# Other prices in a list scheduler: table loads, transfer landings and GpSimd's wake-up

## The chip, the cores and the metric

The kernel runs on one core of one Trainium2 chip. The metric is device microseconds of one execution. A core has five engines that run instruction streams of their own, each in order: TensorE (PE; its weight loads are shown apart as PEld), VectorE (DVE), ScalarE (ACT), GpSimd (POOL) and SyncE (SP), which in this kernel issues every transfer between DRAM and the core's memory (SBUF). TensorE writes to PSUM, of which the kernel uses eight banks of 128 x 512 floats.

## The reference

One layer of an encoder trunk, in float32, for a prompt of 1024 tokens and for 32 further tokens with a cache of 512 past ones; both share the weights.

```python
u = rmsnorm(h, g_pre) @ w_in                  # 1024 -> 4096: qA kA vA gA qB kB vB gB
# A: band attention, 8 heads of 64; a chunk of 64 queries reads its own chunk and 8 before it
s = q @ k.T * 64 ** -0.5 + bias_table[clip(k_pos - q_pos, -128, 128)]
oA = softmax(where(in_band, s, -1e30)) @ v
# B: stick-breaking attention, 8 heads of 64, strictly causal
z = q @ k.T * 64 ** -0.5
log_1m = where(causal, log_sigmoid(-z), 0)
after = reverse_cumsum(log_1m) - log_1m
oB = where(causal, exp(log_sigmoid(z) + after), 0) @ v
y = concat(oA * silu(gA), oB * silu(gB)) @ w_out
h = h + rmsnorm(y, g_post)
h = h + sigmoid(h @ w_ple_gate) * (p @ w_ple)
```

It returns `h` of both groups and their new keys and values.

## The kernel before

**Arithmetic.** Matmuls run on a rounded 32-bit type. To keep float32 precision, an operand is split into a high part (a rounding copy, mostly on ScalarE) and a low part (operand minus high part, on VectorE or GpSimd), and a product is the sum of two or three matmuls. In tile names `h` and `l` stand for these, as in `wTh` and `wTl`.

**Stages.** First the norm and transposes of the input (`ptx`) and a part of the `p @ w_ple` products (`ple`). Then the projections of `w_in`, one matmul group `mm_..` per 128 output columns and 352 tokens, woven together with the attention: 16 heads in eight pairs, in the order A0, B0, A1, B1, ... A3, B3. A head is named by group, pair and half: A01 is the second head of band pair 0. While the attention runs, GpSimd also forms sums of weight blocks and stores them to DRAM (`oB`, `gB` to `sum_dro`, `sum_drg`), for the two products at the end (`o`, `g`), which use a Strassen-like scheme with seven products. The projections of the gates (`mm_gA`, `mm_gB`) come behind the attention, then the rest of `ple`, then the output products, norms and gate.

**One head.** Its queries stand in eight tiles of 128. For tile i, TensorE computes scores into PSUM (`SA`, `SB`). A band head then has VectorE add the bias and find the minimum (`om<-SA,biasA`, `statA`), and ScalarE the exponential (`be<-om,statA`). A stick-breaking head has ScalarE's sigmoid (`om<-SB`), a running product on VectorE (the scan `om<-om,SB`) and a difference on GpSimd (`be<-om`). ScalarE keeps one function table at a time, so from an exponential to a sigmoid and back the program has a table load. The weights must then be transposed for the product with the values (`PVA`, `PVB`). For six tiles TensorE does that (`ptwA`, `ptwB`), with a cast `wTh<-ptw` on ScalarE and the rest `wTl<-ptw,wTh` on VectorE. Tiles 4 and 6 go another way: VectorE transposes squares of 32 x 32, SyncE stores the tile to DRAM (`swapA<-om`) and loads it back in four strips (`be<-swapA`), and then come the cast `wTh<-be` and the rest `wTl<-be,wTh`. So 32 such swaps lie in the kernel, two a head, and the second half of a head's `PV` product waits for both of its own.

**The order.** Nothing in the program is issued as it is written. Every call goes through a `Recorder`, which notes an `Op` with its engine, its predecessors (by the boxes of the tiles that it reads and writes) and a price from `cost`: the time that it keeps its engine (`busy`) and a delay until its result can be used (`late`). `order` then plays a list schedule. Each engine has a time from which it is free; the engine that can start first takes, of the instructions whose operands are there at that time, the one with the lowest key. The key is a class (for TensorE 0 for attention, 1 for projections that fill in) and the place in the recorded program. The finish of an instruction, plus `SEM` and for a reader on TensorE a `MARGIN` of 400 ns, sets when its readers are ready. `emit` writes out the instructions in the order in which they were taken. The buffers of the pools (three banks for scores, two for transposes, two for `mm`, one for `PV`) are given out in the same order. The prices therefore do not appear in the program; they only decide which instruction stands ahead of which on each engine. As every engine works in order, an instruction whose operands come later than planned holds up all that stand behind it on its engine.

For a transfer (`e == "SP"`), the model keeps SyncE busy for `ISSUE` and sends the data down one line of 320 bytes a ns, or slower where the runs are short.

All instructions in the profile have the line of the call in `emit` (L452 before), so they are told apart by tile names.

Of the kernel before, what the change touches and what calls it, by code (L numbers as in the profile page):

```python
# [8 lines left out]
F32 = mybir.dt.float32  # L9
F32R = mybir.dt.float32r  # L10
AF = mybir.ActivationFunctionType
# [161 lines left out]


class Op:
    __slots__ = ("eng", "what", "args", "kw", "key", "busy", "late", "ready", "left", "after", "at", "size", "shared")


LAND = {"PE": 165, "ACT": 0, "DVE": 0, "POOL": 0, "SP": 0, "CTL": 0}
SEM = 60  # L180
MARGIN = 400
ISSUE = 600
DMA_NS, DMA_RATE, DMA_MARGIN = 1500, 320.0, 2000
DVE_SET, POOL_SET = 137, 110


# [77 lines left out]
class Recorder:  # L264
# [35 lines left out]
    def node(self, eng, what, args, kw, after):  # L300
        o = Op()
        o.eng, o.what, o.args, o.kw, o.after = eng, what, args, kw, after
        o.key = (self.cls if eng == "PE" else self.low, len(self.ops))
        o.shared = False
        self.ops.append(o)
        return o

    def add(self, eng, what, args, kw):
        writes, reads = [], []
        method = what[1] if isinstance(what, tuple) else ""  # L310
        for i, a in enumerate(args):
            if isinstance(a, (View, Raw, Segments)):
                (writes if i == 0 or (method == "tensor_tensor_reduce" and i == 7) else reads).append(a)
        for k, a in kw.items():
            if isinstance(a, (View, Raw, Segments)):
                (writes if k in ("out", "accum_out") else reads).append(a)
        o = self.node(eng, what, args, kw, set())
        for mine, write in ((reads, False), (writes, True)):
            for v in mine:
                b = v.buf  # L320
                hit = False
                for other, box, wrote in b.uses:
                    if other is not o and (write or wrote) and all(p < y and x < q for (p, q), (x, y) in zip(v.box, box)):
                        o.after.add(other)
                        hit = True
                if b.pool is not None:
                    if not hit:
                        o.after.add(b.place)
                    b.pool.ops.append(o)
                b.uses.append((o, v.box, write))  # L330
        o.busy, o.late = self.cost(eng, method, args, kw, writes, reads)
        o.shared = eng == "POOL"
        if eng == "DVE":
            sbuf = [v for v in reads if isinstance(v, (View, Segments)) and not v.buf.psum and v.free() > 4]
            o.shared = len(sbuf) > 1 or (method == "tensor_copy" and len(sbuf) == 1 and not writes[0].buf.psum)

    @staticmethod
    def cost(eng, method, args, kw, writes, reads):

        out = writes[0] if writes else None  # L340
        n = out.free() if isinstance(out, View) else 1
        psum = any(isinstance(v, (View, Segments)) and v.buf.psum for v in reads)
        if eng == "PE":
            if method == "transpose":
                return (109 if args[1].shape[0] > 64 else 62), 165
            return max(109.0, 2.5 + 0.449 * args[2].free()) * (1 if args[2].buf.dtype == F32R else 4), 165
        if eng == "ACT":
            return (60 if psum else 95) + 0.83 * n + (190 if "accum_out" in kw else 0), 105
        if eng == "DVE":
            if method == "tensor_tensor_scan":  # L350
                return 120 + 2.1 * n, 85
            if method == "tensor_copy" and not psum:
                return 70 + 0.53 * n, 85
            if method == "scalar_tensor_tensor":
                return 125 + 1.04 * n, 85
            if method == "tensor_tensor_reduce":
                return 90 + 1.04 * n, 150
            return 70 + 1.04 * n, 85
        if eng == "POOL":
            if method == "tensor_tensor":  # L360
                if n == 1:
                    return 535, 40
                return 170 + (1.77 if out.buf.dtype == F32 else 2.15) * n, 40
            if method == "tensor_scalar":
                return 255 + 0.86 * n, 0
            return 100 + 0.82 * n, 0
        size, run = 4, 0
        for v in (out, args[1]):
            if isinstance(v, View) and v.buf.pool is not None:
                size, run = 4 * v.shape[0] * v.free(), 4 * v.shape[-1]  # L370
        return ISSUE, max(size / DMA_RATE, size / run * (8.5 + 0.0365 * run) / 16)


    def order(self):

        import heapq
        for place, old in self.turns:
            place.after.update(x[0] for x in old.uses)
        users = {id(o): [] for o in self.ops}
        for o in self.ops:  # L380
            o.left, o.ready = len(o.after), 0.0
            for a in o.after:
                users[id(a)].append(o)
        names = ("PE", "ACT", "DVE", "POOL", "SP", "CTL")
        free = dict.fromkeys(names, 0.0)
        soon = {e: [] for e in names}
        now = {e: [] for e in names}
        for o in self.ops:
            if not o.left:
                heapq.heappush(soon[o.eng], (0.0, o.key, id(o), o))  # L390
        out, port, line = [], 0.0, 0.0
        while len(out) < len(self.ops):
            best = None
            for e in names:
                if now[e]:
                    t = free[e]
                elif soon[e]:
                    t = max(free[e], soon[e][0][0])
                else:
                    continue  # L400
                if best is None or t < best[0]:
                    best = (t, e)
            t, e = best
            while soon[e] and soon[e][0][0] <= t:
                _, key, n, o = heapq.heappop(soon[e])
                heapq.heappush(now[e], (key, n, o))
            o = heapq.heappop(now[e])[2]
            if o.shared and e == "DVE" and port > t + DVE_SET:
                held = [x for x in now[e] if not x[2].shared]
                if held:  # L410
                    heapq.heappush(now[e], (o.key, id(o), o))
                    pick = min(held)
                    now[e].remove(pick)
                    heapq.heapify(now[e])
                    o = pick[2]
            o.at = t
            if e == "CTL":
                done = t
            elif e == "SP":
                free[e] = t + o.busy  # L420
                line = max(line, t + o.busy + DMA_NS) + o.late
                done = line + DMA_MARGIN
            else:
                if o.shared:
                    t = max(t, port - (DVE_SET if e == "DVE" else POOL_SET))
                    port = t + o.busy
                free[e] = t + o.busy
                done = t + o.busy + o.late
            out.append(o)
            for u in users[id(o)]:  # L430
                if u.eng == e and e != "SP":
                    r = t if e == "CTL" else free[e] if e == "PE" else done
                else:
                    r = done + (0 if u.eng == "CTL" else SEM + (MARGIN if u.eng == "PE" else 0))
                u.ready = max(u.ready, r)
                u.left -= 1
                if not u.left:
                    heapq.heappush(soon[u.eng], (u.ready, u.key, id(u), u))
        return out
# [18 lines left out]
def stream_step(  # L458
# [79 lines left out]
    def load_w(j):  # L538

        if j >= len(order) or j in raws:  # L540
            return
        kind, p = order[j]
        c0 = NAMES.index(kind) * 512 + p * P
        raws[j] = []
        for kh in range(2):
            raw = wpool.tile([P, 4, P], F32, tag="wr", name=f"wr_{kind}{p}_{kh}", bufs=4)
            dma(raw, w_in[0, kh * 512:(kh + 1) * 512, c0:c0 + P].rearrange("(k p) c -> p k c", p=P))
            raws[j].append(raw)
# [657 lines left out]
    for n in range(-1, 8):  # L1206
        a = len(order)
        if n < 7:
            ab, p = pairs[n + 1]
            order += [(k + ab, p) for k in "kqv"]  # L1210
        for _ in range(share.get(n, 0)):
            order.append(gates.pop(0))
        span.append((a, len(order)))
# [655 lines left out]
```

## Time and profile before

| | us |
|---|---|
| median of three runs | 805.05 (804.86 to 805.52) |
| the profiled execution | 809.23 |
| its span, first to last instruction | 807.4 |
| TensorE busy (matmuls) | 788.0 |
| VectorE busy | 567.9 |
| ScalarE busy | 504.4 |
| GpSimd busy | 432.1 |

In the views, a row of a group gives engine, operation, what is written and read, shape and count, then busy time in us and mean duration in ns, then the idle time of the engine just before them and who ended it. A row of the timeline has the start from the span's first instruction and the length in us, and in brackets the idle time before it with its releaser. A row of the waits names who waited for whom, with the total, the number and the longest. Matmuls overlap, so the duration of one is longer than the distance between two.

### The profile page before, as it was taken

Reading aid. Unit: us, or ns where it says so; the run is one execution under the profiler, and the core shown is the slowest. Engines: PE = TensorE matmul, PEld = TensorE weight load, DVE = VectorE, ACT = ScalarE, POOL = GpSimd, SP = SyncE. Lnnn points to the kernel's source line nnn. Section 1 sums busy time; section 2 is a strip of 40 time slices with the busy share of each in tenths; the row PEclk is TensorE's granted clock in tenths of the full one; section 3 lists DMA queues with packets and bytes.
Section 4 is the critical chain, followed back from the end, with each engine's and each line's share of the span. In section 5 each row is a group of like instructions: output and inputs, shape, how many; then the busy total and the mean of one; then the engine's idle time right before and its main releaser. Section 6 shows DMA issues by size and latency. Waiting matters only on the chain.

```text
span 807.4 us, 14271 instructions
## 1 busy us (share of the span) xinstructions
PE 788.0 (98%) x4646; PEld 722.3 (89%) x4646; DVE 567.9 (70%) x1007; ACT 504.4 (62%) x1061; POOL 432.1 (54%) x503
## 2 busy tenths in 40 slices
PE   8999989999999999999999999999999999999997
PEld 7899989899989999899999989999997777878786
DVE  7626768786588788788886688765435787477655
ACT  5636774676586646795675696543327977877641
POOL 5623655764356668134551236777542549598513
PEclk9999999999999999999999999999999999999999
DMA  8419895667878749854535667765569948869633
GB/s 276 149 45 293 215 253 175 195 185 217 225 225 246 215 121 267 216 146 133 151 81 169 147 175 212 234 199 152 166 207 322 298 147 270 278 218 302 215 108 131
DMA packets 160973, 161.09 MB, mean 199 GB/s; under 512 B 39154, under 2 KB 120794, under 8 KB 160899
## 3 DMA queue, kind: packets, MB, share of 16 engines
q1 hardware_dynamic: 160898, 160.18, 67.1%
q8 instruction: 37, 0.61, 0.3%
q14 instruction: 38, 0.30, 0.1%
HBM read 99.23 MB, written 52.49 MB: 188 GB/s over the span
## 4 chain that ended last, share of the span: by engine, by line
PE 72%; DMA 6%; ACT 6%; POOL 5%; DVE 5%; issue 4%; SPq 2%; DVEq 0%; POOLq 0%; ACTq 0%
PE mm_gA L452 6%; PE mm_gB L452 6%; PE mm_kA L452 5%; PE mm_qA L452 5%; PE mm_qB L452 4%; PE SB L452 3%; PE mm_vA L452 3%; PE PVB L452 3%; PE mm_kB L452 3%; PE PVA L452 3%; PE mm_vB L452 3%; PE SA L452 2%; PE o1P L452 2%; PE g2P L452 2%; PE g3P L452 2%
## 5 line engine op out<-in xcount | busy, mean ns | idle before, releaser
L452 POOL TENSOR_TENSOR be<-om 128x128 f32<-128x128 f32 (+7 forms) x64 | 75.4, 1184 | 64.8 <-DVE om L452 29.0
L452 DVE TENSOR_TENSOR_SCAN om<-om,SB 128x384 f32<-128x384 f32 (+5 forms) x96 | 94.9, 1001 | 9.1 <-ACT om L452 7.4
L452 ACT ACTIVATE om<-SB 128x384 f32<-128x384 f32 (+5 forms) x96 | 44.4, 493 | 36.0 <-DVE SB L452 26.9
L452 ACT ACTIVATE be<-om,statA 128x640 f32<-128x640 f32 (+3 forms) x64 | 44.4, 694 | 18.2 <-DVE statA L452 11.0
L452 DVE TENSOR_TENSOR wTl<-be,wTh 128x640 fp32r<-128x640 f32 (+1 forms) x32 | 37.6, 1175 | 10.3 <-ACT wTh L452 8.8
L452 ACT CAST wTh<-ptwB 128x512 fp32r<-128x512 f32 (+3 forms) x64 | 29.5, 481 | 19.6 <-PE ptwB L452 15.4
L452 DVE TENSOR_TENSOR wTl<-ptwB,wTh 128x512 fp32r<-128x512 f32 (+3 forms) x64 | 33.7, 545 | 10.3 <-ACT wTh L452 7.8
L452 DVE TENSOR_TENSOR wTl<-ptwA,wTh 128x512 fp32r<-128x512 f32 (+2 forms) x64 | 29.8, 483 | 15.7 <-ACT wTh L452 12.5
L452 POOL TENSOR_TENSOR oB<-oB,oB 128x256 f32<-128x256 f32 x32 | 27.7, 882 | 18.6 <-DMA oB<-in_w_out_dram 10.5
L452 DVE STREAM_TRANSPOSE om<-be 128x640 f32<-128x640 f32 (+1 forms) x32 | 28.9, 904 | 9.8 <-POOL be L452 4.9
L452 PE MATMUL SB<-kdB,LB 128*128 128x384 f32 (+5 forms) x96 | 34.0, 357 | 1.6 <-DVE om L452 1.6
L452 DVE CUSTOM_DVE_ANT_0 om<-SA,biasA 128x320 f32<-128x320 f32 (+3 forms) x64 | 29.5, 482 | 7.6 <-PE SA L452 4.4
L452 ACT CAST wTh<-ptwA 128x512 fp32r<-128x512 f32 (+2 forms) x64 | 26.2, 426 | 13.3 <-PE ptwA L452 7.5
L452 PE MATMUL SB<-klB,LB 128*128 128x384 f32 (+5 forms) x96 | 32.9, 345 | 0.0
L452 PE MATMUL SA<-kdA,LA 128*128 128x320 f32 (+2 forms) x96 | 30.2, 325 | 0.7 <-DVE LA L452 0.4
L452 POOL TENSOR_TENSOR sggA<-sggA,oggA 128x352 f32<-128x352 f32 x24 | 23.8, 991 | 11.2 <-DVE sggA L452 10.8
L452 PE MATMUL SA<-klA,LA 128*128 128x320 f32 (+2 forms) x96 | 29.6, 320 | 0.0
L452 ACT CAST wTh<-be 128x640 fp32r<-128x640 f32 (+1 forms) x32 | 25.0, 782 | 6.4 <-DMA swapA<-om 3.3
L452 PE MATMUL ptwB<-ident,be 128*128 128x128 f32 x192 | 28.7, 273 | 0.0
L452 PE MATMUL ptwA<-ident,be 128*128 128x128 f32 x160 | 26.3, 276 | 2.0 <-ACT be L452 1.8
L452 DVE TENSOR_TENSOR SB<-SB,maskb 128x128 f32<-128x128 f32 x64 | 17.3, 287 | 13.5 <-PE SB L452 13.1
L452 POOL TENSOR_TENSOR klA<-stkA,kdA 64x1024 fp32r<-64x1024 f32 x8 | 20.7, 2587 | 8.2 <-ACT kdA L452 7.7
(707 smaller groups left out, 2650.5 us busy)
## 6 DMA issues: line engine op xcount, KB each, us to landing
swapA<-om SPq DMA_DIRECT2D x16, 320.0 KB, 2.8
be<-swapA SPq DMA_DIRECT2D x64, 80.0 KB, 3.9
oB<-in_w_out_dram SPq DMA_DIRECT2D x16, 256.0 KB, 4.9
sum_dro<-oB SPq DMA_DIRECT2D x16, 256.0 KB, 3.3
gB<-in_w_ple_gate_dram SPq DMA_DIRECT2D x16, 256.0 KB, 4.6
sum_drg<-gB SPq DMA_DIRECT2D x16, 256.0 KB, 3.8
x<-in_x_prompt_dram SPq DMA_DIRECT2D x16, 256.0 KB, 5.2
h_dr<-h SPq DMA_DIRECT2D x8, 512.0 KB, 3.3
```

Source lines behind the costliest of these rows:

```text
L452: getattr(getattr(tc.nc, o.what[0]), o.what[1])(*args, **kw)
```

## The change

Only prices of the scheduler's model change; no call of the kernel is added, removed or altered.

- ScalarE and VectorE instructions are given 30 ns more each, and GpSimd's `tensor_tensor` too.
- An exponential or sigmoid that follows the other one on ScalarE keeps the engine for 1310 ns more (`TABLE_NS`), and its result is later by as much.
- A transfer keeps SyncE for 500 ns instead of 600. Its data enter the line at once when it is issued, instead of 1500 ns later, and have landed 2050 ns after the line is through with them (`LANDING`), instead of 2000.
- A reader on GpSimd is ready 90 ns later than before.

```diff
@@ class Op
-    __slots__ = (..., "size", "shared")
+    __slots__ = (..., "size", "shared", "table")
-ISSUE = 600
-DMA_NS, DMA_RATE, DMA_MARGIN = 1500, 320.0, 2000
+ISSUE = 500
+DMA_RATE, LANDING = 320.0, 2050
+TABLE_NS = 1310
@@ Recorder.node
-        o.shared = False
+        o.shared, o.table = False, None
@@ Recorder.add
+        o.table = next((a for a in args if a in (AF.Exp, AF.Sigmoid)), None) if eng == "ACT" else None
@@ Recorder.cost
-            return (60 if psum else 95) + 0.83 * n + (190 if "accum_out" in kw else 0), 105
+            return (90 if psum else 125) + 0.83 * n + (190 if "accum_out" in kw else 0), 105
         if eng == "DVE":
             if method == "tensor_tensor_scan":
-                return 120 + 2.1 * n, 85
+                return 150 + 2.1 * n, 85
             if method == "tensor_copy" and not psum:
-                return 70 + 0.53 * n, 85
+                return 100 + 0.53 * n, 85
             if method == "scalar_tensor_tensor":
-                return 125 + 1.04 * n, 85
+                return 155 + 1.04 * n, 85
             if method == "tensor_tensor_reduce":
-                return 90 + 1.04 * n, 150
-            return 70 + 1.04 * n, 85
+                return 120 + 1.04 * n, 150
+            return 100 + 1.04 * n, 85
         if eng == "POOL":
             if method == "tensor_tensor":
                 if n == 1:
-                    return 535, 40
-                return 170 + (1.77 if out.buf.dtype == F32 else 2.15) * n, 40
+                    return 565, 40
+                return 200 + (1.77 if out.buf.dtype == F32 else 2.15) * n, 40
@@ Recorder.order
             elif e == "SP":
                 free[e] = t + o.busy
-                line = max(line, t + o.busy + DMA_NS) + o.late
-                done = line + DMA_MARGIN
+                line = max(line, free[e]) + o.late
+                done = line + LANDING
             else:
...
                 free[e] = t + o.busy
-                done = t + o.busy + o.late
+                if o.table and o.table != table:
+                    table = o.table
+                    free[e] += TABLE_NS
+                done = free[e] + o.late
...
-                    r = done + (0 if u.eng == "CTL" else SEM + (MARGIN if u.eng == "PE" else 0))
+                    r = done + (0 if u.eng == "CTL" else SEM + (MARGIN if u.eng == "PE" else 90 if u.eng == "POOL" else 0))
```

More of the change, by code (lines that the diff above doesn't have):

```diff
@@ L175 @@
 class Op:
-    __slots__ = ("eng", "what", "args", "kw", "key", "busy", "late", "ready", "left", "after", "at", "size", "shared")
+    __slots__ = ("eng", "what", "args", "kw", "key", "busy", "late", "ready", "left", "after", "at", "size", "shared", "table")
 LAND = {"PE": 165, "ACT": 0, "DVE": 0, "POOL": 0, "SP": 0, "CTL": 0}
@@ L390, in order @@
                 heapq.heappush(soon[o.eng], (0.0, o.key, id(o), o))
-        out, port, line = [], 0.0, 0.0
+        out, port, line, table = [], 0.0, 0.0, None
         while len(out) < len(self.ops):
```

## The prediction

> **What bounds the kernel now.** I read the page's busy times first, then the chain that ended last, then TensorE's own waits, and last the waits behind those.
>
> ```profile
> span 807.4 us, 14271 instructions
> PE 788.0 (98%) x4646; PEld 722.3 (89%) x4646; DVE 567.9 (70%) x1007; ACT 504.4 (62%) x1061; POOL 432.1 (54%) x503
> ...
> PE 72%; DMA 6%; ACT 6%; POOL 5%; DVE 5%; issue 4%; SPq 2%; DVEq 0%; POOLq 0%; ACTq 0%
> ```
>
> The same chain in order of time (start, length, what):
>
> ```profile
> 587.33 21.50 PE mm_gB L452 x133
> ...
> 649.07 2.78 PE o1P L452 x12
> ```
>
> TensorE is busy for 788.0 of 807.4 us and carries 72% of the chain. In its long stretches it does nothing but issue: 133 matmuls of 352 columns in 21.50 us are 161 ns each, 12 of 512 columns in 2.78 us are 230 ns, about 0.45 ns a column. The change neither adds nor removes an instruction: both built programs have the same ones on every engine, ten table loads among them. So only the time in which TensorE waits can change. The view of its waits says who ended them:
>
> ```profile
> PE PVA L452 <- ACT wTh L452: 2.7, 1, 2.7
> PE ptx L452 <- DVE be L452: 2.4, 2, 1.3
> PE ptwA L452 <- ACT be L452: 1.8, 2, 1.3
> PE SB L452 <- DVE om L452: 1.6, 3, 0.9
> PE idle L452 <- DVE newh L452: 1.3, 1, 1.3
> PE ptkA L452 <- DVE wTl L452: 1.3, 1, 1.3
> ...
> PE o0P L452 <- ACT A12o L452: 0.5, 1, 0.5
> PE SA L452 <- DVE LA L452: 0.4, 1, 0.4
> ...
> PE g0P L452 <- DMA hh<-h_dr: 0.3, 1, 0.3
> ```
>
> The columns are total us, number, longest. With the four rows left out (0.5, 0.4, 0.3 and 0.3 us) they come to 13.8 us. This is nearly all that a better order can win, apart from the reduced clock that one of them brings.
>
> **What the change moves.** The scheduler keeps the recorded order as its priority and lets an instruction go when its model says that the operands are there. Three prices change.
>
> First, ScalarE, VectorE and most GpSimd instructions get 30 ns more, and a change between the exponential and the sigmoid gets 1310 ns:
>
> ```profile
> L452 ACT ACT_TABLE_LOAD x10 | 12.8, 1283 | 1.1 <-PEq L1857 0.7 <-DVE statA L452 0.3
> ```
>
> One of them in the timeline:
>
> ```profile
> 474.55 1.28 ACT L452 ACT_TABLE_LOAD   x1
> 475.85 0.83 ACT L452 ACTIVATE be<-om,statA 128x640 f32<-128x640 f32 x1
> ...
> 477.63 0.44 PE L452 MATMUL ptwA<-ident,be 128*128 128x128 f32 x2 [1.29 <-ACT be L452]
> ```
>
> The load costs ScalarE 1.28 us, and here the transposes behind it stood 1.29 us on TensorE, because the order of before did not know of it. I count the matmul work (0.45 ns a column) that the two orders put between an operand's producer and its reader; where the new order has more of it than the wait was long, I take the wait as gone.
>
> - The last row above is A31, tile 5: its transposes now stand 18.2 us behind their scores instead of 15.7. The pair of extra table loads moves from there to A11, where the same distance is 17.0 instead of 10.5. Both waits of the row "ptwA <- ACT be" go: -1.8 us.
> - The bank of `ptkA` came free late, after this:
>
> ```profile
> 147.28 2.82 DVE L452 TENSOR_TENSOR wTl<-be,wTh 128x640 fp32r<-128x640 f32 x1 [1.02 <-ACT wTh L452]
> ...
> 151.44 0.27 PE L452 MATMUL ptkA<-ident,stkA 128*32 128x128 f32 x1 [1.30 <-DVE wTl L452]
> ```
>
> In the new order VectorE empties that bank (`wTl<-ptwB`) ahead of the 2.82 us split, not behind it: -1.3 us.
> - "SB <- DVE om": the scores wait for a bank that the scan holds. The longest (B11, tile 4) has 4.5 us between the bank's last writer and itself instead of 3.6. Over the attention, score tiles with under 2.5 us of such distance fall from 48 to 38, transposes from 47 to 43: -1.2 of 1.6 us.
> - `o0P2` now comes after `o1P1` (-0.5), `S2g` ahead of GpSimd's `h` rows (-0.3), `SA` two matmuls of 161 ns later (-0.3), the two `ptx` one matmul later each, 0.23 and 0.16 (-0.4).
>
> Sum of what goes: -5.8 us. From the projection of the gates at 560 us on, TensorE's order is otherwise almost the same, so this is settled in the attention.
>
> Second, transfers. An 80 KB leg of the swap through DRAM was modelled as 600 + 1500 + 250 + 2000 ns = 4.35 us from issue to landing, now as 500 + 250 + 2050 = 2.80; 256 KB falls from 4.9 to 3.35, 320 KB from 5.1 to 3.55. Measured (the page's transfers):
>
> ```profile
> swapA<-om SPq DMA_DIRECT2D x16, 320.0 KB, 2.8
> be<-swapA SPq DMA_DIRECT2D x64, 80.0 KB, 3.9
> oB<-in_w_out_dram SPq DMA_DIRECT2D x16, 256.0 KB, 4.9
> ```
>
> The columns are count, size of one and median us to landing. The view of the tile `swapA` gives the issue (min/median/max ns) and the spread:
>
> ```profile
> L452 SPq DMA_DIRECT2D be<-swapA x64: 302/432/1227, 85.5 to 485.9; - x64
> ...
> DMA to landing us min/median/max: 2.0/3.9/7.2
> ```
>
> The issue (432 ns) and the way out (2.8 us) support the new price. The way back (median 3.9) and the weights (4.9) do not: there the old one had the median, and the new one is 1.1 to 1.6 us short. What is lost is cover. On ScalarE the cast `wTh<-be` moves up by 2.0 us of matmul work on the mean of 32 swaps, and a cast that stands too early holds up the ScalarE queue behind it, evacuations of banks among them; `PV` of the head's second half follows at once. Where the transfers are dense this shows already in the kernel of before:
>
> ```profile
> 103.31 0.72 ACT L452 CAST wTh<-be 128x640 fp32r<-128x640 f32 x1 [3.30 <-DMA swapA<-om]
> ...
> 104.08 0.65 PE L452 MATMUL PVA<-wTh,v2A 128*128 128x512 f32 x1 [2.73 <-ACT wTh L452]
> ```
>
> The group of these casts (count, busy us, mean ns, idle time before them and who ended it):
>
> ```profile
> L452 ACT CAST wTh<-be 128x640 fp32r<-128x640 f32 x24 | 17.4, 726 | 4.9 <-DMA swapA<-om 3.3 <-DMA be<-swapA 1.3 <-PE PVB L452 0.2
> ```
>
> By stages (busy time of the engines, then clock, DMA share, GB/s):
>
> ```profile
> 60.00:120.00 60.00, 56.78 (x358) 54.71 (x357) 40.65 (x90) 41.87 (x90) 29.95 (x38) 0.97 0.93 254
> ...
> 104.00:107.00 3.00, 2.92 (x10) 2.82 (x11) 2.11 (x4) 3.00 (x7) 1.64 (x4) 0.55 1.06 256
> 107.00:110.00 3.00, 3.00 (x21) 2.82 (x21) 1.21 (x2) 2.90 (x7) 0.10 (x1) 0.88 1.02 280
> ```
>
> From 60 to 120 us the DMA engines are busy for 0.93 of the time. This wait (A00) stays: it has 27.0 us of matmul work from scores to `PV`, where it had 26.5. A01 behind it loses 2.1 us (24.0 to 21.9), and its last legs stand three issues earlier, worth 1 us: +1.1, with some of it at a lower clock +1.5. For B11 the legs now stand ahead of a transfer of 512 KB, so no loss. For the other 13 heads I allow +1.0 in all. The lower bound of both together is 0; the upper is two more waits like the 2.7 us one, each with its clock. The clock was 0.55 and 0.88 in the two stretches of 3 us behind it, which takes 3 x 0.45 + 3 x 0.12 = 1.7 us more: 2 x 4.4 = +8.8.
>
> Third, GpSimd's wake-up of 90 ns ahead of its instructions only moves their modelled results back; GpSimd is busy for 54%, and readers that stand later have the matmuls of the projections in front of them. Zero, within -0.5 and +0.5. New waits of the whole reshuffle (nearest rows: the shortest of the list, 0.3 to 0.5 us each, three of them): +1.0.
>
> **Sum.** -5.8 + 1.5 + 1.0 + 1.0 = -2.3 us. The profiled execution took 809.23 us (its span of 807.4 and 1.8 around it) and would take 806.9; the median of the runs, 805.05, is 4.2 us below it, and with the same difference it becomes 802.7.
>
> **A rule weighed.** Between the end of the load above (475.83) and the exponential (475.85) lie 0.02 us, so the trace shows no cost beside the 1.28 us. The Trainium skill (ScalarE: Activation LUTs, What ACT_TABLE_LOAD costs) adds a drain of about 1.38 us to every switch; by it the 1310 ns would be half the price, and the waits at the switches would stay. That would take the 1.8 us out of the sum: 804.5. The rows speak against it, so it gets 0.03.
>
> **The rivals.**
> - *The cover is missed* (slower). Swap legs land later than the 2.8 us that the model now gives, the cast stands at the head of ScalarE's queue, and `PV` waits. For it: 3.9 us median, 7.2 at most, the 3.30 us wait above. Against: 24 of the 32 casts together waited 4.9 us in the run before, 3.3 of them in the one case shown, so most have cover, and a leg's price falls by 1.55. It decides once the lost cover costs over 6.4 us (-5.8 + 1.0 + 6.4 = +1.6); at its upper bound it is -5.8 + 8.8 + 1.0 = +4.0, 809.1. Chance 0.28. The Trainium skill (TensorE: Matmul & The Clock Gate, Part 1) has the clock halve after an idle window of about 3.4 us; the row with 0.55 shows that a wait of 2.7 us can be enough.
> - *The waits change places* (no change). New waits of the sizes listed add up to what goes: 805. For it: the list of before is made of single events of 0.3 to 2.7 us, as any order leaves some. Chance 0.19, the case of the rule included.
> - *Also the long wait goes*. If the leg of the first head lands before its reader, 2.7 and 1.7 us go too, and A01 keeps its cover: -2.3 - 4.4 - 1.5 = -8.2, 796.9. Chance 0.10.
> - That the model charges table loads and yet saves none is certain (ten in both); it is in the forecast.
>
> **Numbers.** The forecast has 0.43. Faster by over 0.2% (1.6 us, about what a measurement of this kernel can tell from no change): 0.43 + 0.10 = 0.53; within: 0.19; slower: 0.28. The forecast's own range is 800 to 803.4. The range of 8 in 10 takes in the case of the long wait and most of the missed cover: 796.5 to 810. The predicted time is 802.7 us.
>
> **What would show it.** In the profile after, TensorE's waits should sum to 11 or 12 us; the rows "ptwA <- ACT be" and "ptkA <- DVE wTl" should be gone, "PVA <- ACT wTh" should stand at 2.7 us or more, and ScalarE should wait longer for `be<-swapA` and `be<-swapB`. I am wrong if `PV` waits in heads beyond the first two, if a second stretch of lower clock appears, or if the row "SB <- DVE om" grows.

## The result: slower by about 8 us

| | before | after |
|---|---|---|
| median of five runs, us | 805.14 (804.86 to 805.64) | 813.07 (809.91 to 813.46) |
| ratio of the times | | 1.0086 (1.0070 to 1.0103) |
| a profiled execution, us | 809.23, and a second one 805.04 | 809.91, the shortest of the five |
| its span | 807.4, and 803.3 | 807.8 |

The change is slower, by 0.86%; 802.7 us was predicted, and 813.07 lies outside the range of 796.5 to 810. The profiles have to be read with care: the one of before that the prediction used was of a long execution (809.23), the one of after is of the shortest, 3.2 us under its median. So a second profile of the unchanged kernel was taken in the experiments (the run same, 805.04 us, close to the median), and after is compared with that one. This shows 4.5 us of span where the medians differ by some 8 us; the rest of the loss is not seen in this profile.

The page of after has the same matmuls:

```profile
span 807.8 us, 14282 instructions
PE 785.4 (97%) x4646; PEld 720.9 (89%) x4646; DVE 573.4 (71%) x1007; ACT 506.3 (63%) x1061; POOL 437.3 (54%) x503
...
PE 73%; DMA 10%; POOL 6%; DVE 3%; ACT 3%; issue 2%; SPq 2%; ACTq 0%; POOLq 0%; DVEq 0%
```

In the chain that ended last, the share of transfers is 10%, against 6% and 4% in the two profiles of before. TensorE's waits in after (total us, number, longest):

```profile
PE PVA L457 <- ACT wTh L457: 4.5, 3, 2.3
PE PVB L457 <- ACT wTh L457: 1.5, 2, 1.1
PE SA L457 <- DVE statA L457: 1.4, 2, 1.0
PE idle L457 <- DVE newh L457: 1.3, 1, 1.3
PE ptx L457 <- DVE be L457: 1.2, 2, 0.9
PE ptwA L457 <- DVE wTl L457: 0.9, 2, 0.6
PE SA L457 <- DMA klA<-klA: 0.9, 1, 0.9
...
PE SB L457 <- DVE om L457: 0.5, 1, 0.5
```

and in the second profile of before:

```profile
PE ptwA L452 <- ACT be L452: 1.8, 2, 1.3
PE ptx L452 <- DVE be L452: 1.7, 2, 0.9
PE SB L452 <- DVE om L452: 1.6, 3, 0.9
PE ptwA L452 <- DVE wTl L452: 1.4, 1, 1.4
PE idle L452 <- DVE newh L452: 1.3, 1, 1.3
PE ptkA L452 <- DVE wTl L452: 1.3, 1, 1.3
...
PE PVA L452 <- ACT wTh L452: 0.5, 1, 0.5
```

The rows that the prediction wanted gone are gone or shorter (`ptwA` for `be`, `ptkA`, `SB` for `om`). In their place `PVA` and `PVB` wait 6.0 us for the cast `wTh`, in heads A10, B11, A20, A31 and B30. The longest of them in the timeline (A20):

```profile
342.62 0.72 ACT L457 CAST wTh<-be 128x640 fp32r<-128x640 f32 x1 [2.85 <-DMA be<-swapA]
...
343.38 0.82 DVE L457 TENSOR_TENSOR wTl<-be,wTh 128x640 fp32r<-128x640 f32 x1 [3.40 <-ACT wTh L457]
343.40 0.85 PE L457 MATMUL PVA<-wTh,v2A 128*128 128x512 f32 x4 [2.25 <-ACT wTh L457]
```

ScalarE stood for 2.85 us at a cast whose transfer had not landed, VectorE for 3.40 us behind that, TensorE for 2.25. The group of all 32 casts, in the second profile of before and in after (count, busy us, mean ns, idle time of ScalarE in front of them, and who ended it):

```profile
L452 ACT CAST wTh<-be 128x640 fp32r<-128x640 f32 (+1 forms) x32 | 25.0, 782 | 5.4 <-DMA be<-swapA 3.7 <-DMA be<-swapB 1.4 <-PE PVB L452 0.2
```

```profile
L457 ACT CAST wTh<-be 128x640 fp32r<-128x640 f32 (+1 forms) x32 | 25.0, 780 | 19.1 <-DMA be<-swapA 9.1 <-DMA be<-swapB 8.7 <-PE PVB L457 1.1
```

5.4 us have become 19.1. That the swap as a whole got slower is not the cause. The two ways of a band swap, first in the second profile of before, then in after (count, size of one, median us to landing):

```profile
swapA<-om SPq DMA_DIRECT2D x16, 320.0 KB, 2.9
be<-swapA SPq DMA_DIRECT2D x64, 80.0 KB, 3.6
```

```profile
swapA<-om SPq DMA_DIRECT2D x16, 320.0 KB, 3.7
be<-swapA SPq DMA_DIRECT2D x64, 80.0 KB, 2.9
```

The way out became slower and the way back faster; together they are 6.5 and 6.6 us. The view of the whole tile `swapA` in after has the spread:

```profile
DMA to landing us min/median/max: 2.0/3.4/6.2
```

This last view mixes four kinds of transfers. The trace tells the landing of only some of them: 27 of the 64 legs `be<-swapA` in after took 2.0 to 6.2 us, ten in the first profile of before 2.0 to 4.5.

**An account of the stalls.** For the experiments I took from each trace all distances between the starts of neighbouring matmuls, less the usual distance for that shape, one value for all runs. What is over is called a stall; a stretch at a lower clock counts as one too. The matmuls are the same, so the span less the sum of these stalls has to be one number by the way it is made: it is 778.6 us in 17 of the 20 profiles (778.7 to 779.5 in the others). Each stall over 0.25 us was then followed back, through its releaser or the instruction before it on the same engine, up to 8 us; it is put down to a transfer if this chain ends at one. Between the second profile of before and after, stalls put down to legs of the swap grow from 2.2 to 11.0 us, to other transfers from 2.2 to 5.2; those put down to none fall from 9.2 to 4.6. The stalls under 0.25 us, 11.1 and 8.4 us, are put down to nothing. The sums are firm; the split is rougher, because a chain can often be followed back in more than one way. In dma_alone below, for example, another rule for the step back gives the swap 16.8 us and the other transfers 9.2, where the table has 10.1 and 14.2; for after it gives 11.5 and 4.0.

### The profile page after: what moved, and what is told of

It is laid out like the page before. It is cut to its first block, busy times and chain, and to the rows that moved or that the text cites. A ratio compares the mean times of both kernels' runs of the same rounds, so it can differ in the third digit from the quotient of the medians.

```text
span 807.8 us, 14282 instructions
## 1 busy us (share of the span) xinstructions
PE 785.4 (97%) x4646; PEld 720.9 (89%) x4646; DVE 573.4 (71%) x1007; ACT 506.3 (63%) x1061; POOL 437.3 (54%) x503
## 4 chain that ended last, share of the span: by engine, by line
PE 73%; DMA 10%; POOL 6%; DVE 3%; ACT 3%; issue 2%; SPq 2%; ACTq 0%; POOLq 0%; DVEq 0%
PE mm_gB L457 6%; PE mm_gA L457 5%; PE mm_vA L457 5%; PE mm_qB L457 4%; PE mm_qA L457 4%; PE PVB L457 4%; PE mm_vB L457 4%; PE mm_kA L457 4%; PE SB L457 3%; PE PVA L457 3%; DMA be<-swapA 3%; PE mm_kB L457 3%; PE SA L457 3%; SPq L457 2%; PE g0P L457 2%
## 5 line engine op out<-in xcount | busy, mean ns | idle before, releaser
L457 POOL TENSOR_TENSOR be<-om 128x128 f32<-128x128 f32 (+7 forms) x64 | 78.4, 1231 | 56.5 <-DVE om L457 33.6
L457 DVE TENSOR_TENSOR_SCAN om<-om,SB 128x384 f32<-128x384 f32 (+5 forms) x96 | 95.2, 1003 | 10.8 <-ACT om L457 7.0
L457 ACT CAST wTh<-ptwB 128x512 fp32r<-128x512 f32 (+3 forms) x64 | 29.6, 481 | 20.0 <-PE ptwB L457 15.1
L457 DVE TENSOR_TENSOR wTl<-ptwA,wTh 128x512 fp32r<-128x512 f32 (+2 forms) x64 | 30.0, 482 | 15.1 <-ACT wTh L457 12.1
L457 ACT CAST wTh<-be 128x640 fp32r<-128x640 f32 (+1 forms) x32 | 25.0, 780 | 19.1 <-DMA be<-swapA 9.1
L457 POOL TENSOR_TENSOR gB<-gB,gB 128x256 f32<-128x256 f32 x32 | 26.1, 838 | 17.1 <-DMA gB<-in_w_ple_gate_dram 11.5
L457 POOL TENSOR_TENSOR oB<-oB,oB 128x256 f32<-128x256 f32 x32 | 24.9, 799 | 19.1 <-DMA oB<-in_w_out_dram 13.0
L457 ACT CAST wTh<-ptwA 128x512 fp32r<-128x512 f32 (+2 forms) x64 | 26.1, 424 | 10.8 <-PE ptwA L457 7.3
L457 POOL TENSOR_TENSOR klB<-stkB,kdB 64x1024 fp32r<-64x1024 f32 x8 | 19.2, 2395 | 13.5 <-ACT kdB L457 13.5
```

Of the source, the lines that this page charges most:

```text
L457: getattr(getattr(tc.nc, o.what[0]), o.what[1])(*args, **kw)
```

## The experiments

Theory 1 after the result, in the texts below also called cover: the new landing is too short, so readers stand too early and hold up the engine on which they wait. Theory 2: any new price gives another order, and the time falls where it falls. A run with `SEM` at 61 ns instead of 60 has otherwise the same prices and another order; it is called a second draw. A third question came up on the way: what is a wait worth if it alone is taken away? All numbers are in one table. A ratio is to the kernel before as it was measured beside that run; "idle" is ScalarE's idle time in front of the casts of swapped tiles, and the last three columns are the account above, all in us.

| run | median | ratio to before (95%) | idle | swap | other transfers | none |
|---|---|---|---|---|---|---|
| same | 804.7 | 0.9994 (0.9978 to 1.0009) | 5.4 | 2.2 | 2.2 | 9.2 |
| after | 813.1 | 1.0086 (1.0070 to 1.0103) | 19.1 | 11.0 | 5.2 | 4.6 |
| dma_alone | 828.6 | 1.0275 (1.0242 to 1.0308) | 21.2 | 10.1 | 14.2 | 12.5 |
| all_but_dma | 805.2 | 1.0008 (0.9994 to 1.0022) | 8.8 | 4.6 | 2.2 | 7.8 |
| sem_61 | 811.0 | 1.0076 (1.0053 to 1.0099) | 5.8 | 3.1 | 2.6 | 12.6 |
| after_pv_later | 815.8 | 1.0135 (1.0112 to 1.0159) | 20.1 | 10.1 | 8.7 | 5.0 |
| swap_legs_old | 807.0 | 1.0033 (1.0012 to 1.0054) | 5.6 | 0.0 | 9.7 | 8.8 |
| rest_old | 807.4 | 1.0032 (1.0018 to 1.0046) | 23.4 | 7.1 | 1.5 | 9.6 |
| after_sem_61 | 813.2 | 1.0104 (1.0077 to 1.0130) | 17.2 | 10.8 | 9.6 | 5.8 |
| landing_3600 | 807.1 | 1.0029 (1.0016 to 1.0042) | 5.4 | 4.4 | 1.6 | 11.2 |
| landing_5000 | 824.4 | 1.0251 (1.0227 to 1.0276) | 1.4 | 0.3 | 10.0 | 20.0 |
| all_but_dma_sem_61 | 806.4 | 1.0017 (1.0003 to 1.0031) | 9.1 | 4.0 | 5.5 | 7.9 |
| table_alone | 807.8 | 1.0041 (1.0025 to 1.0058) | 5.6 | 0.5 | 3.0 | 11.3 |
| before_waits_later | 815.1 | 1.0127 (1.0104 to 1.0149) | 1.9 | 0.5 | 6.8 | 13.5 |
| after_casts_later | 839.7 | 1.0413 (1.0391 to 1.0435) | 10.5 | 5.0 | 13.1 | 25.8 |
| dma_alone_sem_61 | 825.7 | 1.0260 (1.0220 to 1.0300) | 21.2 | 11.0 | 14.2 | 6.9 |
| landing_2800 | 801.8 | 0.9955 (0.9940 to 0.9970) | 15.1 | 6.5 | 3.0 | 2.9 |
| landing_2800_sem_61 | 801.4 | 0.9966 (0.9949 to 0.9983) | 11.1 | 4.1 | 4.2 | 2.9 |
| landing_3100 | 802.6 | 0.9965 (0.9951 to 0.9978) | 10.7 | 2.5 | 5.4 | 6.9 |

**Which part of the change, and how much is chance.** The unchanged kernel again:

> The kernel before, unchanged, with a new profile. All theories: 805.1 us within 0.5. Its profile shows a usual execution; the one shown before the prediction took 809.2 us, so some waits of that profile (the 2.7 us one of PVA and the stretch at half clock are the first candidates) should be missing or shorter here, 3 to 4 us in all.

804.7 us. The 2.7 us wait of A00 is 0.5 us here: it differs between executions of one program.

The transfer prices alone, the rest alone, and a price that says nothing:

```diff
 # dma_alone: the kernel before, with
-ISSUE = 600
-DMA_NS, DMA_RATE, DMA_MARGIN = 1500, 320.0, 2000
+ISSUE = 500
+DMA_RATE, LANDING = 320.0, 2050
 # all_but_dma: the changed kernel with these lines (and order's) the other way round
 # sem_61: the kernel before, with
-SEM = 60
+SEM = 61
```

> The kernel before with the new prices of transfers alone (issue 500 ns, entry at once, landing 2050 ns). Theory 1, the cover is missed: readers of swap legs stand too early, so 809 to 814 us, with PVA and PVB waiting for the cast wTh for 5 us or more in several heads. Theory 2, scatter: any new price gives another order of some 40% of the instructions, and the time falls anywhere between 803 and 815 us, with waits of no particular kind.

> The changed kernel with the old prices of transfers (600, 1500 and 2000 ns); the table loads, the 30 ns and the wake-up stay. Theory 1, the cover is missed: the cover is back, so at most 805 us (800 to 805), and the waits of PVA and PVB for the cast wTh sum to under 3.5 us. Theory 2, scatter: anywhere between 803 and 815 us.

> The kernel before with SEM at 61 ns instead of 60, and nothing else: a change of a price that says nothing of the chip. Theory 1, the cover is missed: within 1.5 us of 805.1, as every transfer keeps its price. Theory 2, scatter: the order changes at 2038 of 4648 places of TensorE, as many as in the whole change, and the time differs from 805.1 by several us, 808 to 813 as likely as not.

All of the loss is in the transfer prices: without them the rest of the change is worth 805.2 us, nothing. Alone they cost 24 us, more than either theory had. What the longest waits there look like, three lines of dma_alone show: the cast waits for its strip, and the copy `sumrowA` behind it on ScalarE, which TensorE needs, waits with it.

```profile
113.89 0.72 ACT L452 CAST wTh<-be 128x640 fp32r<-128x640 f32 x1 [3.73 <-DMA be<-swapA]
114.52 0.25 ACT L452 COPY sumrowA<-ptsA 8x128 f32<-8x128 f32 x1
...
114.82 0.33 PE L452 MATMUL ptwA<-ident,be 128*128 128x128 f32 x1 [3.19 <-ACT sumrowA L452]
```

But theory 2 holds too, by a part: one ns in `SEM` moved 2038 places of TensorE and cost 6 us; of 4.7 us of new stalls 3.4 go back to no transfer. The order of before is the better one of its pair. So some later questions were asked of two orders. The runs with a single order (swap_legs_old, rest_old, table_alone, and the landings of 3100, 3600 and 5000) can be off by as much as this pair.

**Which transfers.** In the changed kernel only the legs of the swap, or only all others, get a landing as long as before:

```diff
-                done = line + LANDING
+                done = line + (3600 if swap else LANDING)    # swap_legs_old
+                done = line + (LANDING if swap else 3600)    # rest_old
```

> The changed kernel, but the legs of the swap have landed 3600 ns after the line is through with them, which gives the 4.35 us from issue to landing that the kernel before had; every other transfer keeps the new 2050 ns. Theory 1, the cover of the swap is missed: the cover is back, 805 us (803 to 808), and the stalls of TensorE that can be followed back to a leg of a swap fall from 11.0 us to under 5. Theory 2, scatter: anywhere between 803 and 829 us, and no tie to the swap.

> The counterpart: the legs of the swap keep the new 2050 ns, every other transfer lands after 3600 ns. Theory 1, the cover of the swap is missed: the stalls stay, 811 us or more, over 8 us of them followed back to legs of swaps. Theory 2, scatter: anywhere between 803 and 829 us.

> The changed kernel with SEM at 61 ns instead of 60, so another draw of an order under the same new prices. Theory 1: as the prices of transfers decide, 809 to 829 us, with over 8 us of stalls followed back to legs of swaps. Theory 2, scatter: as likely under as over 811 us, and under 806 in one draw of three.

The stalls follow the prices: long legs leave no stall of the swap and 9.7 us of others, long others leave 7.1 us of the swap and 1.5. Each half alone brings back 6 us, so theory 1 in its narrow form, the swap alone, fell: rest_old was expected at 811 or more and took 807.4. Nor are the two halves parts of a sum: with both, in landing_3600 below, the time is 807.1 us, no better than with either. The casts of rest_old wait most of all (23.4 us), which costs less than I had thought; it seems that not every cast has somebody behind it whom TensorE needs:

```profile
L459 ACT CAST wTh<-be 128x640 fp32r<-128x640 f32 (+1 forms) x32 | 25.0, 780 | 23.4 <-DMA be<-swapA 13.2 <-DMA be<-swapB 8.3 <-PE PVB L459 1.8
```

The second draw of the changed kernel came out like the first, 813.2 and 813.1. Against its own partner, the kernel before with `SEM` at 61 (811.0), it is only 2 us slower: the whole change cost 8 us in one draw and 2 in the other. What holds in both draws is the part of the transfer prices, 8 and 7 us (all_but_dma took 805.2 and, in a second draw that comes below, 806.4).

**Is it the place of the reader?** In after_pv_later the second half of `PV` of the five stalled heads stands up to 16 projection matmuls later, with all else in place:

> The changed kernel with its own order on every engine, except that on TensorE the second half of PV in five heads (A10, B11, A20, A31, B30), whose waits for the cast of a swapped tile cost 1.0, 1.4, 2.4, 1.6 and 0.6 us in its profile (6.9 us), stands behind up to 16 projection matmuls that followed it; where something that is needed soon depends on it, it moves by fewer (2 matmuls in A10, 1 matmul and a pair of scores in B11). Theory 1, readers of swapped tiles stand too early: 0.3 + 0.4 + 2.4 + 1.6 + 0.5 = 5 us go, 808 us (807 to 809.5), and the waits stay gone. Theory 2, scatter: the waits come up again a little later behind the same transfers, at the next reader or on ScalarE, and the time stays within 2 us of 813.

815.8 us: theory 1 failed as I had put it, and the time is a little over what theory 2 had. What happened at A31, in the timeline:

```profile
487.49 0.72 ACT L478 CAST wTh<-be 128x640 fp32r<-128x640 f32 x1 [2.17 <-DMA be<-swapA]
488.12 0.48 ACT L478 ACTIVATE om<-SB 128x384 f32<-128x384 f32 x1
...
488.51 0.44 ACT L478 COPY stvB<-mm_vB 128x352 f32<-128x352 f32 x1
...
489.00 0.28 PE L478 MATMUL ptvB<-ident,stvB 128*32 128x128 f32 x1 [2.15 <-ACT stvB L478]
```

`PV` no longer waits, but `stvB`, queued behind the cast on ScalarE, is late, and TensorE waits 2.15 us for it instead. The wait sits where the cast is. So the casts were moved too (in A01, A10, A11, B11, A20, A31, B30 by 2 to 5 instructions of ScalarE in the trace, with most of their low parts and `PV`):

> The changed kernel with its own order, except that of the casts of swapped tiles that waited for their transfer by 0.5 us or more in its profile, those of nine tiles stand 2 to 4 instructions later on ScalarE, most of their low parts 1 to 4 later on VectorE, and the second half of PV of those heads 7 to 22 projection matmuls later on TensorE. Theory 1, the casts that stand too early hold up what is behind them: the idle time of ScalarE in front of the casts falls from 19.1 us to under 8, the stalls of TensorE that go back to legs of swaps from 11.0 to under 5, and the time from 813 to 807 us (805 to 809). Theory 2: the stalls move on to other readers, as when PV alone was moved, and the time stays within 2 us of 813.

839.7 us, far worse than either theory had. The idle time fell (19.1 to 10.5) and the swap's stalls too (11.0 to 5.0), near to what was expected, but the stalls put down to no transfer went from 4.6 to 25.8. The same was tried on the kernel before, where eight groups with waits of 7.9 us in all were moved behind projections:

> The kernel before with its own order on every engine, except that on TensorE eight groups that waited in its second profile stand 4 to 12 projection matmuls later: the second half of PV in A00 (0.7 us), transposes of A01 tile 5 (1.5), ptkA1 (1.5), transposes of A11 tile 5 (0.7), scores of B10 tile 3 (0.5) and B11 tile 4 (1.1), transposes of A31 tile 5 (1.4), scores of B30 tile 5 (0.5): 7.9 us. Theory 1, a wait is worth its length where a projection can stand in for it: 797 to 800 us. Theory 2, the reader behind it waits in its place, as in the run with PV moved in the changed kernel: within 2 us of 805.

815.1 us: 10 us lost where a gain of 5 to 8 was expected. Waits of the next in line took their place, in the view of the waits:

```profile
PE ptwA L505 <- DVE wTl L505: 4.3, 6, 2.0
PE SB L505 <- DMA wr_qA<-in_w_in_dram: 2.1, 1, 2.1
PE ptosA L505 <- ACT sumrowA L505: 1.8, 1, 1.8
PE ptsA L505 <- DVE sumsA L505: 1.4, 1, 1.4
```

A transpose that waits is itself the producer for a cast, a rest and a bank; put later, it makes these late, and no other engine's order was moved with it. So in these three runs a wait of the list was not worth its length. That it would be, if the orders of the other engines moved along, is not shown.

**How long a landing?** The changed kernel with other values of one constant (2050 in the change), and two more draws:

```diff
-DMA_RATE, LANDING = 320.0, 2050
+DMA_RATE, LANDING = 320.0, 2800    # and 3100, 3600, 5000
```

> The changed kernel with LANDING at 3600 ns instead of 2050, for every transfer: from issue to landing as long as in the kernel before (4.35 us for a leg of the swap), the rest of the change as it is. Theory 1, cover: the stalls of TensorE that go back to a transfer fall from 16 us or more (changed kernel, and its draw with SEM 61) to under 9, and the time is 805 us (803 to 808). Theory 2, scatter alone: anywhere between 803 and 829 us.

> The changed kernel with LANDING at 5000 ns, longer than all but a few measured landings need. Theory 1, cover: the stalls that go back to a transfer stay under 7 us and the time is 800 to 805 us; if more cover costs elsewhere (heads end later, and the projections that fill in run out before them), 805 to 810 us, with new stalls between 480 and 560 us. Theory 2, scatter alone: anywhere between 803 and 829 us.

> The changed kernel with LANDING at 2800 ns, half way between the 2050 of the change and the 3600 that is like before. Theory 1, cover: the idle time of ScalarE in front of the casts of swapped tiles lies between the 19.1 us of the changed kernel and the 5.4 us of LANDING 3600, at 9 to 15 us, and the time at 806 to 812 us. Scatter alone: the idle time follows the landing all the same, the time does not, 803 to 829 us.

> The changed kernel with LANDING at 2800 ns and SEM at 61 ns: another draw of an order beside the one that took 801.8 us. Theory 1, a landing priced near the measured median is the best: 800 to 805 us, 9 to 16 us of idle time in front of the casts of swapped tiles, and under 6 us of stalls that go back to no transfer. Theory 2, the 801.8 us were a lucky order: 805 to 811 us.

> The changed kernel with LANDING at 3100 ns. Theory 1: between its neighbours at 2800 (801.8 us) and 3600 (807.1 us): 802 to 806 us, 5 to 15 us of idle time in front of the casts. Theory 2, scatter of some 3 us to both sides: anywhere between 801 and 811 us.

> The changed kernel with the old prices of transfers, and SEM at 61 ns: another draw of an order beside the one that took 805.2 us. Theory 1, cover: 802 to 809 us, under 9 us of stalls that go back to a transfer. Theory 2, scatter alone: anywhere between 803 and 829 us. It also says whether the table loads, the 30 ns and the wake-up gain anything under the old prices of transfers: a gain of 2 us or more would have to show in both draws.

In order of the landing: 2050 ns 813.1 and 813.2 us, 2800 ns 801.8 and 801.4, 3100 ns 802.6, 3600 ns 807.1, 5000 ns 824.4. I had expected the time at 2800 between its neighbours (806 to 812 us); it has its least there, and two orders of this landing lie within 0.4 us of each other, so it is hardly a lucky draw. The second draw with all old prices of transfers, 806.4 us, belongs with the 805.2 of the first (its stalls that go back to a transfer, 9.5 us, are a little over the 9 expected). landing_2800 is faster than both kernels, by 0.45% (0.30 to 0.60%) than the one before. From the short side the casts wait; from the long side others do. At 5000 ns, in one order, the casts hardly wait any more,

```profile
L457 ACT CAST wTh<-be 128x640 fp32r<-128x640 f32 (+1 forms) x32 | 25.0, 780 | 1.4 <-DMA be<-swapA 0.8 <-PE PVB L457 0.2 <-DMA be<-swapB 0.2
```

and TensorE waits for the weights of the output product, whose loads came late (ScalarE stood 5.20 us for one of them), and in the attention:

```profile
PE o0P L457 <- ACT oB L457: 7.5, 2, 6.5
PE PVB L457 <- ACT wTh L457: 4.1, 2, 2.7
PE ptwA L457 <- ACT sumrowA L457: 2.1, 1, 2.1
```

I had expected 800 to 805 us there, or 805 to 810; both were wrong. That order has 14 table loads instead of ten, 5.1 us more on ScalarE, so not all of its loss need come from transfers. In landing_2800 one long wait is left, that of A00:

```profile
PE PVA L457 <- ACT wTh L457: 4.5, 2, 3.5
PE ptx L457 <- DVE be L457: 1.8, 3, 1.2
PE idle L457 <- DVE newh L457: 1.3, 1, 1.3
```

**Two left-overs.** The table loads alone, and a second draw of the transfer prices alone:

> The kernel before with the price of the table loads alone. By the prediction the two waits of the transposes for the exponential behind a table load go, 1.8 us: 803 us. By scatter 803 to 813 us: both waits gone all the same, and others in their place. By theory 1, cover, not over 811 us, as the transfers keep their prices.

> The kernel before with the new prices of transfers alone and SEM at 61 ns: another draw beside the one that took 828.6 us. Theory 1, short landings cost some 8 us and the rest of the 24 us was an unlucky order: 810 to 818 us, with 15 us or more of stalls that go back to transfers. Rival, without the price of the table loads short landings cost 20 us or more in any order: 823 us or more. If cover does not decide: also under 808.

With the table loads priced, both waits of the transposes behind a load are gone, as predicted, and the time is 2.4 us longer all the same: `mm_kB` waits 1.7 us for the cast of its weights, and others with it. The new order also has two table loads more, where the prediction had ten in any case:

```profile
L457 ACT ACT_TABLE_LOAD x12 | 15.4, 1283 | 0.9 <-PEq L1862 0.7
```

The 24 us of dma_alone were no unlucky order (825.7 us in the second, 15 us over the kernel before with the same `SEM`). That short landings cost more without the other new prices (24 and 15 us in the two draws) than with them (8 and 7) is measured; why is not settled. In both draws of dma_alone 14.2 us of stalls are put down to transfers other than the swap, against 5.2 and 9.6 with the other prices.

## Why the prediction was wrong, step by step

- *Only TensorE's waits can change.* Right as far as it goes: the matmuls are the same in every order. The account above does not test it, because its 778.6 us are one number by the way it is made. The list of 13.8 us was not nearly all that an order can win or lose: the stalls of that profile are 28.8 us, some 13 of them in pieces under 0.25 us. The waits, expected at 11 or 12 us, sum to 17.2 in the view of after.
- *The waits that go, -5.8 us.* Right in the changed kernel: the named rows are gone or shorter, and stalls put down to no transfer fell from 9.2 to 4.6, in landing_2800 to 2.9. That close agreement is in part luck: one ns in `SEM` raised the same sum by 3.4. Nor do the runs bear out that a wait taken away is time won: where TensorE's readers alone were moved, the time rose by 10 us. Under the old prices of transfers the table loads, the 30 ns and the wake-up gain nothing in one draw (805.2 us) and 4.6 in the other (806.4 against 811.0), so whether they gain by themselves is open.
- *Transfers, +1.5 for the first two heads and +1.0 for the other 13.* This is the term that failed. Stalls that go back to legs of the swap grew by 8.8 us, nearly all in the other heads; the upper bound was 8.8, and I took 2.5. I had measured cover as the mean of 32 swaps (2.0 us lost), and found it enough because the median leg (3.9 us) was hidden before. But the casts stand in the order of a queue: the late ones decide, up to 6.2 us against a price of 2.80, and each holds up all behind it. In after the median leg took 2.9 us, almost its new price, and the casts waited 19.1 us all the same. I also priced the reader `PV` alone, not the evacuations behind the cast, though the text named them.
- *What was read off the transfers.* The 7.2 us named as the longest way back is of another transfer of the tile (`stvA<-swapA`); the longest leg `be<-swapA` that the trace of before tells took 4.5, the longest `be<-swapB` 5.6. And the way out, 2.8 us before, took 3.7 in after, over its new price of 3.55.
- *Other transfers.* I costed none of them. By the account they add 3.0 us in the profile of after and 7.4 in its second draw (there against same). With their old landing alone (rest_old) 6 us of the loss come back, as with that of the swap alone; how much of the loss is theirs cannot be told, as the two do not add up.
- *A00's wait stays.* Wrong, and not to be predicted: it was 2.7 us in one profiled execution of before, 0.5 in another, none in that of after, 3.5 in that of landing_2800.
- *GpSimd's wake-up, zero.* Not tested apart; nothing in the runs speaks against it. In the trace of after GpSimd starts 73 ns (median of 141 waits) after the event that releases it, ScalarE and VectorE 23 and 24.
- *The rule on table loads.* With 1310 ns as the price of a load, the row "ptwA <- ACT be" is gone in after and in table_alone. In after each load but the first begins 0.02 us after the instruction before it, and the exponential or sigmoid 0.01 us after the load (once 0.45 us). The Trainium skill (ScalarE: Activation LUTs, What ACT_TABLE_LOAD costs) would have had it stay, for want of a further 1.38 us; the trace does not agree.
- *The rivals.* "The cover is missed" is what happened, with the signs that the prediction had named: `PV` waits in heads beyond the first two. The other two signs, a second stretch of lower clock and a longer row "SB <- DVE om", did not come. Its price of 809.1 us was 4 us short; the transfers that it left out add 3.0 us in the profile of after, but that is an execution of 809.91, so the 4 us are not fully accounted for. "New waits of the whole reshuffle", +1.0, had no firm ground: one ns in `SEM` cost the kernel before 6 us.
- *The size of the range.* 796.5 to 810 took in 4 us for the missed cover and no scatter of the order itself.

## What to carry to other kernels

In an order that a model plans, a transfer that is priced too short can cost more than its own delay, because its reader stands at the head of an in-order queue; here a price far too long (5000 ns) cost as much and more. So sweep that one constant before anything else: here it was worth 11 us between 2050 and 2800 ns, more than the whole change. The best price of a leg here, 3.55 us, is near the median of `be<-swapA` in the unchanged kernel (3.9 and 3.6 us in its two profiles). But the median moves with the order: it was 2.9 us in after, where a price of 2.80 was too short, and 2.7 in landing_2800. Before believing any difference of a re-planned order, run the same prices with one of them a nanosecond off.

## What the runs showed of the hardware that was not expected

The way from an 80 KB leg's issue to its landing has a wide spread in one kernel (`be<-swapA`, of the legs whose landing the trace tells: 2.0 to 6.2 us in after, 2.0 to 4.5 before), and a wait that hangs on a swap (A00) is 2.7 us in one execution of a program and 0.5 in another; these two executions took 809.2 and 805.0 us. In landing_2800 the granted clock fell behind A00's wait of 3.5 us as it did behind the 2.7 us one before (third last column):

```profile
100.00:103.00 3.00, 0.07 (x1) 0.00 (x0) 0.00 (x0) 0.16 (x1) 1.33 (x2) 1.00 0.92 256
103.00:106.00 3.00, 2.38 (x8) 2.19 (x9) 1.63 (x3) 3.00 (x7) 1.19 (x1) 0.62 1.08 320
106.00:109.00 3.00, 3.00 (x19) 2.83 (x18) 0.27 (x2) 1.03 (x4) 0.20 (x4) 0.81 0.89 244
```

So this execution of landing_2800 (803.33 us, the longest of its six) lost some 3.5 us to that wait and, as an estimate from the two last rows, 1.7 to the clock (3 x 0.38 + 3 x 0.19); whether an earlier first head would win them was not tried. The length of a wait alone does not tell whether the clock falls. In sem_61 a wait of 2.09 us, at 116.5 us, was enough:

```profile
116.00:119.00 3.00, 2.49 (x10) 2.36 (x11) 2.46 (x6) 1.86 (x5) 2.93 (x5) 0.57 0.68 188
```

In dma_alone the wait of 3.19 us shown above was not:

```profile
114.00:117.00 3.00, 2.18 (x14) 2.16 (x15) 2.32 (x6) 2.56 (x5) 0.00 (x0) 1.00 1.02 256
117.00:120.00 3.00, 2.24 (x15) 1.82 (x13) 1.12 (x2) 0.67 (x3) 2.62 (x4) 1.00 0.48 108
```
